# S5 parameters, attention keys, gate rows and S5 copies moved to other places in a hybrid attention and S5 layer

## Chip, cores and metric

The kernel runs on one core of a Trainium2 chip. The metric is the device time of one execution in microseconds (us). The engines are TensorE (PE), VectorE (DVE), ScalarE (ACT), GpSimd (POOL) and SyncE (SP, which issues DMAs). Each works through its own instructions in order and waits on semaphores for the others.

## The reference

One layer of a streaming encoder on 1024 prompt tokens and 64 sample tokens, width 1024, everything in float32. Cut to its steps:

```python
mod = silu(c) @ w_mod + b_mod                      # 1024 x 3072
shift, scale, gate = mod[:, :D], mod[:, D:2*D], mod[:, 2*D:]
h = rms_norm(x, g_norm) * (1 + scale) + shift
z = h @ w_in                                       # 11 column groups
zq, zk, zv, zqi, zki, zwi, zga, zu, zgs, zma, zmb = split_cols(z)
score = sum over heads of wi * relu(qi . ki)       # index scores, rotated qi, ki
keep the top n_sel (256, or 144 for the sample) admissible keys per query
o = softmax(q . k / 8 over the kept keys) @ v      # 8 heads, 2 key heads
branch_a = (o * silu(zga)) @ w_attn_proj
y_ssm, state = s5(zu, lambda, dt, b, c, d_skip)    # complex diagonal scan
g = gelu(y_ssm) @ w_glu                            # 512 -> 1024
branch_b = (g[:, :512] * sigmoid(g[:, 512:]) * silu(zgs)) @ w_ssm_proj
merged = sigmoid(zma) * branch_a + sigmoid(zmb) * branch_b
y = rms_norm(x + gate * (merged @ w_out), g_final)
```

## The kernel before

Every product in float32 is made of three: both operands are split into a rounded high part and the rest (`hhi`, `hlo`, `whi`, `wlo`), and PE adds hi by hi, lo by hi and hi by lo (`mm3_parts`, L197 to L206). A weight split is a DMA into one of two `raw` buffers, a cast on ACT and a subtract on POOL or DVE (`load_split`, L157; `rest_on[0]` says which).

The stages follow each other as PE runs them:

1. **Modulation** (to about 33 us). `w_mod` comes in sixteen slabs. Seven of them are split (`wmh` on ACT, `wml` on DVE), the others are multiplied as they are. The columns of `gate` are left for later.
2. **Turn** (to 107 us). Each of nine token tiles is normed, transposed, scaled (`ht`), split into `hhi` and `hlo` (the subtract of `hlo` on POOL, L557), and projected to index keys (`chunk_a`). `ssm_params`, a generator, works out the S5 parameters in small steps on DVE; before, `next(params, None)` takes one step per tile from tile 2 on.
3. **Index scores and top-k** (to about 277 us on DVE). DVE finds a threshold for each query by counting, makes a mask (`bias`) and flags for blocks that need an exact selection. PE adds up the flags (L948), DVE turns the sum into `arm_i`, and a branch runs `select` for such a block. PE meanwhile runs `kv` and the projection `jobs`: `late` is the queue of these jobs, each of three chunks of 384, 384 and 320 tokens (`products`). Four are queries (`q_d`), four are S5 inputs (`u_d`), then the merge gates (`ma_d`, `mb_d`), and so on. Before, `N_TOPK = 18` steps of `late`, each half a chunk, are run ahead of `topk`, and `beside[0] = gates()` takes one step of the gate product after each chunk: 32 matmuls with the columns of `gate` (L1156).
4. **Attention** (to about 552 us). `build_keys` transposes and splits the keys (`kst`), `att_queries` fetches the first block of queries. Attention is woven with `late`, one step for each of its own (`R_ATT`).
5. **S5** (to about 670 us). `ssm_in` makes the local states `zs`, `ssm_scan` (DVE) runs the scan, `ssm_fix` adds the carries and copies the last states to `fin`, `ssm_out_tables` and `ssm_out` make the outputs. It is woven with `late` at 3.2 steps for each of its own.
6. **Rest of `late`, GLU, branch projections, output.** GLU weights come in pairs by `load_pair`; the result goes to `yhi` and `ylo`. POOL makes `olo` at the start of the GLU (L1516).

The chunks of `late` end in one of two accumulator banks (`acc`, two buffers), which ACT empties (`st`, L609). A scheduler places each engine's instructions, so the order below is its order and not that of the source.

Of the kernel before, what the change touches and what calls it, by code (L numbers as in the profile page):

```python
# [24 lines left out]
F32 = mybir.dt.float32  # L25
# [25 lines left out]
N_TOPK = 18  # L51
# [12 lines left out]
MB = 3  # L64
PAR0 = 2
# [15 lines left out]
def hybrid_step(ctx, tc, ins, outs):  # L81
# [108 lines left out]
    beside = [None]  # L190
# [125 lines left out]
    def ssm_params(sp):  # L316
# [88 lines left out]
        doublings(a8re, a8im, 0)  # L405
        yield
# [262 lines left out]
    ix_ctx = ExitStack()  # L669
# [7 lines left out]
    scores[8] = ixp.tile([P, 576], F32, tag="scs", name="scs", bufs=1)  # L677

    relu_turn = [0]
    sums = ixp.tile([P, 2, 7], F32, name="sums", bufs=1)  # L680
# [85 lines left out]
    def k_of(b):  # L766
        return K_SEL - extra.get(b, 0)
# [80 lines left out]
    tkc = ixp.tile([P, 6, 7], F32, name="tkc", bufs=1)  # L848
    tks = ixp.tile([P, 10, 7], F32, name="tks", bufs=1)
    near_v = ixp.tile([P, 7, NEAR], F32, name="near_v", bufs=1)  # L850
    iota = ixp.tile([P, NEAR], F32, name="iota", bufs=1)
    flags = ixp.tile([P, 14], F32, name="flags", bufs=1)
    fl = ixp.tile([1, 4, 14], F32, name="fl", bufs=1)
    arm_i = ixp.tile([1, 1], I32, name="arm_i", bufs=1)
    ones = ixp.tile([P, 1], F32, name="ones", bufs=1)
    low_f = ixp.tile([P, 1024], BF16, name="low_f", bufs=1)

    def topk_constants():
# [24 lines left out]
        pool.memset(tks[64:P, 9, 6:7], -(bias_w[8] - k_of(8)) * BIG)  # L883
        pool.memset(near_v[64:P, 6], 0.0)

    def topk():
# [14 lines left out]
        for p in range(N_COUNT):  # L901
            now, old = e[p % 2], e[(p + 1) % 2]
            for b in BLOCKS:
                nq, n, i = tok_tile(b)[1], bias_w[b], COL[b]
                c = slice(i, i + 1)
                m = ixp.tile([P, 1024], BF16, tag="gt", name="gt", bufs=2)[:nq, :n]
                dve.tensor_scalar(m, scores[b][:nq], t[:nq, c], -(k_of(b) - (NEAR + 1) / 2), op0=OP.is_ge, op1=OP.add,
                                  accum_out=now[:nq, c])
                if p == N_COUNT - 1:
                    y = ixp.tile([P, 1024], F32, tag="relu", name="below")[:nq, :n]  # L910
# [21 lines left out]
        oh = ixp.tile([P, 7, NEAR], F32, name="oh", bufs=1)  # L932
# [21 lines left out]
        gt = ixp.tile([P, 1024], BF16, tag="gt", name="gts", bufs=2)  # L954
        rk = ixp.tile([P, 1024], F32, tag="relu", name="rank")
# [36 lines left out]
    def att_queries(b):  # L992
        t0, nq = tok_tile(b)

        qt = atp.tile([P, 4, P], F32, tag="qt", name="qt", bufs=1)
        sync.dma_start(qt[:, :, :nq], q_d[:, :, t0:t0 + nq].rearrange("m p t -> p m t"))
        tab = atp.tile([P, 2, P], F32, tag="tab", name="tab", bufs=1)
# [7 lines left out]
        st = atp.tile([P, 4, 2, P], F32R, tag="qs", name="qs")  # L1005
# [133 lines left out]
    run(chunks_b)  # L1139
    inadmissible()  # L1140
    def gates():


        yield
        ps = big()
        for h in range(0, D, 512):
            for k in range(0, KD, 2):
                whi = wpool.tile([P, 2, 512], F32R, tag="whi", name="ghi")
                wlo = wpool.tile([P, 2, 512], F32R, tag="wlo", name="glo")
                v = w_mod[k * P:(k + 2) * P, 2 * D + h:2 * D + h + 512].rearrange("(k p) c -> p k c", p=P)  # L1150
                for i in range(2):
                    load_split(whi[:, i:i + 1], wlo[:, i:i + 1], v[:, i:i + 1])
                yield
                for i in range(2):
                    for j, w in enumerate((whi, wlo)):
                        pe.matmul(ps[0:4, h:h + 512], c4[:, k + i, :], w[:, i], start=(k + i + j == 0),  # L1156
                                  stop=(k + i + j == KD))
                yield
        r = wpool.tile([4, D], F32, tag="whi", name="grow")
        act.copy(r, ps[0:4])  # L1160
        sync.dma_start(grow_d, r)
        for h in range(0, D, 512):
            hs = slice(h, h + 512)
            g = wpool.tile([2, 2, 512], F32, tag="wlo", name="gsum")
            sync.dma_start(g[:, 0:2], grow_d[:, hs].rearrange("(i b) c -> b i c", b=2))
            pool.tensor_tensor(g[:, 0], g[:, 0], g[:, 1], op=OP.add)
            sync.dma_start(g[:, 1], ins["b_mod"][:, 2 * D + h:2 * D + h + 512].to_broadcast([2, 512]))
            pool.tensor_tensor(g[:, 0], g[:, 0], g[:, 1], op=OP.add)
            sync.dma_start(gate_d[:, hs], g[:, 0])
        yield  # L1170
# [9 lines left out]
    beside[0] = gates()  # L1180
# [6 lines left out]
    run(topk())  # L1187
    rest_on[0] = pool
    run(beside[0])
    ix_ctx.close()  # L1190

# [3 lines left out]
    kst = rb.tile([P, 2, 2, 1024], F32R, tag="t2", name="kst")  # L1195

    qw = wpool.tile([P, 4, P], F32, tag="ub", name="qw", bufs=1)
    pool.memset(qw, 0.0)

    def heads():  # L1200
        pt = tokp.tile([P, 2, 2, 4, 2, P], F32R, tag="wtok", name="pt")
        build_keys(kst, None, [(ktok[:, t], P) for t in range(8)])
        keys, vals = kst, [vst]
        with tc.issue_after(q_stored.ins):
            ready = att_queries(BO[0])
        other = None
        for i, b in enumerate(BO):
            if b == 8:
                ck = atp.tile([P, 4, P], F32, tag="qt", name="ck", bufs=1)
# [4 lines left out]
            for h in range(8):  # L1214
# [4 lines left out]
                if h == VH and b == 8:  # L1219
                    cv = atp.tile([P, 4, 2, 64], F32, tag="qt", name="cv", bufs=1)  # L1220
# [58 lines left out]
    act.mul(arf[:, 1, 16:32], a8im, -1.0)  # L1279
    ca_t, tq_t = {}, {}  # L1280

    def ssm_out_tables(q):
# [101 lines left out]
    def ssm_fix(q):  # L1384
# [98 lines left out]
    rest_on[0] = dve  # L1483
    nxt = load_pair(*pairs[0])
# [184 lines left out]
```

## Time and profile before

| | us |
|---|---|
| median of 3 runs (1076.43 to 1077.16) | 1077.0 |
| profiled execution | 1080.46 |
| its span (first to last instruction) | 1077.8 |
| PE busy | 989.8 |
| DVE busy | 660.6 |
| ACT busy | 497.5 |
| POOL busy | 314.6 |

The times of all rows come from the one profiled execution and count from its span's start. A row of a timeline gives the start, the duration, the engine, the line, the operation, output and inputs, the shape, and in brackets how long the engine was idle before it and what ended that. Instructions of one engine overlap a little, so that the step from one start to the next says what one costs in a row of equal ones. Lines are those of the kernel before.

### The profile page before, as it was taken

The numbers are of one execution on the slowest core, as the hardware profiler recorded it, in microseconds if no ns is written. First come the engines' busy times: TensorE is split into PE (matmuls) and PEld (weight loads), VectorE is DVE, ScalarE is ACT, GpSimd is POOL, SyncE is SP. The second block draws the span as 40 slices with busy tenths as digits, with TensorE's granted clock in tenths as the row PEclk, the third lists the DMA queues.
The fourth block names the chain that finished last, engine by engine and source line by source line (L and its number), as shares of the span: only waits on it lengthen the run. The fifth ranks groups of instructions, "written<-read, shape, count | busy, mean of one in ns | idle before, by whom it ended". The sixth has DMA issues, their size and how long they took to land. (4 is left out here: it accounts for less than half of the span.)

```text
span 1077.8 us, 16668 instructions
## 1 busy us (share of the span) xinstructions
PE 989.8 (92%) x5910; PEld 893.7 (83%) x5910; DVE 660.6 (61%) x1478; ACT 497.5 (46%) x1034; POOL 314.6 (29%) x456
## 2 busy tenths in 40 slices
PE   7766999999979999999989948999899999999997
PEld 1565777998868899998878947999899999998786
DVE  3596888899278788876556996110323566564243
ACT  3654577322269778887614102223431344442122
POOL 2565102444454312211142715533123000001200
PEclk9887999999999899999999987999999999999999
DMA  8711301134533212113293304465432345444133
GB/s 307 213 51 55 89 1 47 40 92 130 124 80 78 69 33 58 48 54 87 42 154 82 98 11 121 121 143 115 158 107 93 89 153 164 145 121 156 52 129 113
DMA packets 142009, 108.43 MB, mean 101 GB/s; under 512 B 33126, under 2 KB 128912, under 8 KB 141924
## 3 DMA queue, kind: packets, MB, share of 16 engines
q1 hardware_dynamic: 140404, 105.08, 35.1%
q10 hardware_dynamic: 1232, 2.23, 0.6%
q8 instruction: 46, 0.75, 0.3%
q14 instruction: 39, 0.32, 0.1%
q0 software_dynamic: 288, 0.05, 0.0%
HBM read 77.81 MB, written 25.19 MB: 96 GB/s over the span
## 5 line engine op out<-in xcount | busy, mean ns | idle before, releaser
L200 PE MATMUL acc<-hhi,whi 128*128 128x384 f32 (+1 forms) x768 | 259.3, 342 | 10.0 <-ACT whi L154 4.0
L201 PE MATMUL acc<-hlo,whi 128*128 128x384 f32 (+1 forms) x768 | 255.8, 337 | 0.0
L205 PE MATMUL acc<-hhi,wlo 128*128 128x384 f32 (+1 forms) x768 | 150.4, 335 | 14.8 <-POOL wlo L155 14.8
L200 PEld LDWEIGHTS acc<-hhi,whi 128*128 128x128 f32 x768 | 148.6, 193 | 13.5 <-ACT whi L154 4.6
L201 PEld LDWEIGHTS acc<-hlo,whi 128*128 128x128 f32 x768 | 148.7, 194 | 1.3 <-issue 0.4
L205 PEld LDWEIGHTS acc<-hhi,wlo 128*128 128x128 f32 x768 | 131.0, 191 | 16.7 <-POOL wlo L155 15.7
L155 POOL TENSOR_TENSOR wlo<-raw,whi 128x512 fp32r<-128x512 f32 x64 | 91.3, 1441 | 179.8 <-ACT whi L154 143.8
L609 ACT COPY st<-acc 128x384 f32<-128x384 f32 (+1 forms) x60 | 27.5, 459 | 93.2 <-PE acc L205 76.5
L154 ACT CAST whi<-raw 128x512 fp32r<-128x512 f32 x64 | 38.4, 620 | 56.7 <-PE acc L205 23.9
L1069 DVE TENSOR_TENSOR pt<-tp,pt 128x512 fp32r<-128x512 f32 (+3 forms) x112 | 56.6, 520 | 12.3 <-ACT pt L1068 10.8
L1604 POOL TENSOR_TENSOR yh<-yh,gfin 128x512 f32<-128x512 f32 (+1 forms) x9 | 11.6, 1287 | 174.5 <-ACT xr L1600 174.5
L1040 ACT ACTIVATE pm<-pm,mx 128x1024 f32<-128x1024 f32 (+8 forms) x72 | 56.0, 779 | 12.5 <-DVE mx L1033 12.3
L1030 PE MATMUL sc<-kst,qs 128*128 128x512 f32 (+3 forms) x192 | 54.8, 364 | 4.8 <-issue 4.4
L200 PE MATMUL acc<-wohi,mhi 128*128 128x512 f32 (+2 forms) x152 | 57.8, 384 | 0.0
L201 PE MATMUL acc<-wolo,mhi 128*128 128x512 f32 (+2 forms) x152 | 57.5, 383 | 0.0
L1064 PE MATMUL tp<-ident,pm 128*128 128x128 f32 (+2 forms) x328 | 53.4, 272 | 2.6 <-DVE pm L1048 1.5
L1033 DVE CUSTOM_DVE_ANT_0 pm<-sc,bias 128x512 f32<-128x512 f32 (+4 forms) x72 | 43.1, 598 | 18.5 <-PE sc L1030 15.1
L1068 ACT CAST pt<-tp 128x512 fp32r<-128x512 f32 (+3 forms) x112 | 48.8, 450 | 12.2 <-PE tp L1064 10.8
L1081 PE MATMUL o<-pt,vst 128*128 128x256 f32 x288 | 49.0, 296 | 2.4 <-ACT pt L1068 1.6
L1064 PEld LDWEIGHTS tp<-ident,pm 128*128 128x128 f32 (+2 forms) x328 | 38.6, 140 | 12.1 <-issue 5.2
L705 DVE SCALAR_TENSOR_TENSOR sc<-relu,wi,sc 128x512 f32<-128x512 f32 (+5 forms) x42 | 43.2, 1031 | 4.1 <-ACT relu L703 1.3
L1081 PEld LDWEIGHTS o<-pt,vst 128*128 128x128 f32 x288 | 40.3, 192 | 6.5 <-DVE pt L1069 2.7
(476 smaller groups left out, 2271.6 us busy)
## 6 DMA issues: line engine op xcount, KB each, us to landing
raw<-in_w_in SPq DMA_DIRECT2D x68, 256.0 KB
wm<-in_w_mod SPq DMA_DIRECT2D x16, 512.0 KB
xt<-in_x_prompt SPq DMA_DIRECT2D x8, 512.0 KB
raw<-in_w_mod SPq DMA_DIRECT2D x16, 256.0 KB
raw<-in_w_out SPq DMA_DIRECT2D x16, 256.0 KB
xr<-in_x_prompt SPq DMA_DIRECT2D x16, 256.0 KB
ma_d<-st SPq DMA_DIRECT2D x16, 192.0 KB
mb_d<-st SPq DMA_DIRECT2D x16, 192.0 KB
```

Of the source, the lines that this page charges most:

```text
L155: rest_on[0].tensor_tensor(lo, raw, hi.bitcast(F32), op=OP.subtract)
L200: pe.matmul(ps, lhi(k), rhi(k), start=(k == 0), stop=False)
L201: pe.matmul(ps, lhi(k), rlo(k), start=False, stop=False)
L205: last_mm[0] = pe.matmul(ps, llo(k), rhi(k), start=False, stop=(k == nk - 1))
L705: dve.scalar_tensor_tensor(scores[b][:nq], r[:nq, :n], w, scores[b][:nq], op0=OP.mult, op1=OP.add, accum_out=sums[:nq, 0, col] if h == 4 e ...
L1030: pe.matmul(ps, self.st[:, self.h // 2, self.h % 2, :nq], self.keys[:, self.h // 4, j, c:c + m], start=(j == 0), stop=(j == 1))
L1033: dve.tensor_tensor_reduce(out=self.pm[:, c:c + m], in0=ps, in1=bias[self.b][:nq, c:c + m], op0=OP.add, op1=OP.min, scale=-0.125, scalar=t ...
L1040: act.activation(self.pm, self.pm, AF.Exp, bias=self.ng, scale=-1.0, accum_out=self.sm)
L1064: pe.transpose(tp[:rows, i, :nq], self.pm[:, c0:c0 + rows], ident[:nq, :nq])
L1068: act.copy(d0, tp[:rows, i0:i1, :nq])
L1069: dve.tensor_tensor(d1, tp[:rows, i0:i1, :nq], d0.bitcast(F32), op=OP.subtract)
L1081: last_mm[0] = pe.matmul(o, v[:rows, kt, pr // 2].rearrange("p a d -> p (a d)"), pk[:rows, j, i, :, :nq], start=(kt == 0 and j == 0), stop ...
```

## The change

Four parts. The parameters' first three steps run within the modulation loop (`PARK`), and the DMA of the S5 matrices becomes a step of its own. `N_TOPK` is 0, and the keys and first queries are made ahead of the branch, in pools of their own. The gate product leaves the chunks and runs in the GLU loop, two steps for each chunk, one 128 x 512 slab per step. In the S5 stage the copies to `fin` go from POOL to ACT, a memset from POOL to DVE, and the second half of `ca` from DVE to POOL.

```diff
-N_TOPK = 18
+N_TOPK = 0
+PARK = (1, 2, 3)
...
                 evac(c, t0, n, ps)
-                if beside[0]:
-                    next(beside[0], None)
...
             if 2 * k + 1 - j == X0:
                 load_x(0)
+        if k in PARK:
+            next(params)
...
+    def gates(gp):
+        ps = [bank1()[0:4], bank1()[0:4]]
+        parts = [(h, k) for h in range(2) for k in range(KD)]
+        def load(h, k):
+            w = [gp.tile([P, 1, 512], F32R, tag=f"gw{i}", name=f"gw{i}") for i in range(2)]
+            load_split(w[0], w[1], w_mod[k * P:(k + 1) * P, None, 2 * D + h * 512:2 * D + h * 512 + 512])
+            return w
+        nxt = load(*parts[0])
+        yield
+        for i, (h, k) in enumerate(parts):
+            w, nxt = nxt, load(*parts[i + 1]) if i + 1 < len(parts) else None
+            for j in range(2):
+                pe.matmul(ps[h], c4[:, k, :], w[j][:, 0], start=(k + j == 0), stop=(k + j == KD))
+            yield
...
-    run(topk())
+    tk = topk(ixp)
+    for _ in range(N_COUNT - 1 + len(BLOCKS) + 1):
+        next(tk)
+    qw = wpool.tile([P, 4, P], F32, tag="ub", name="qw", bufs=1)
+    pool.memset(qw, 0.0)
+    kst = rb.tile([P, 2, 2, 1024], F32R, tag="t2", name="kst")
+    build_keys(kst, None, [(ktok[:, t], P) for t in range(8)])
+    with tc.issue_after(q_stored.ins):
+        ready = att_queries(BO[0])
+    run(tk)
     rest_on[0] = pool
-    run(beside[0])
...
-        dve.scalar_tensor_tensor(ca[:, :, 1], u1, -1.0, u2, op0=OP.mult, op1=OP.subtract)
+        pool.tensor_tensor(ca[:, :, 1], u1, u2, op=OP.subtract)
...
-        pool.tensor_copy(fin[:, 1, :, rs], z4[:, :, rs, 8])
-        pool.tensor_copy(fin[:, 0, :, rs], z4[:, :, rs, NCH])
-        pool.memset(z4[:, :, rs, 8], 0.0)
+        act.copy(fin[:, 1, :, rs], z4[:, :, rs, 8])
+        act.copy(fin[:, 0, :, rs], z4[:, :, rs, NCH])
+        dve.memset(z4[:, :, rs, 8], 0.0)
...
     rest_on[0] = dve
+    gate_gen = gates(ga_ctx.enter_context(tc.tile_pool(name="gap", bufs=2, side="right")))
     nxt = load_pair(*pairs[0])
...
             dve.tensor_tensor(ylo[:, m, t0:t0 + n], s[:, :n], yhi[:, m, t0:t0 + n].bitcast(F32), op=OP.subtract)
+            for _ in range(2):
+                next(gate_gen, None)
...
+    run(gate_gen)
```

PE's order at the flags matmul, before; the last of sixteen chunks since `kv` stands ahead of it, the gate matmuls (L1156) around it, and the transposes of the keys behind it:

```order
L205 MATMUL acc<-hhi,wlo 128x320 x8
L948 MATMUL acc<-flags,ones 1x14
L200 MATMUL acc<-hhi,whi 128x384
L201 MATMUL acc<-hlo,whi 128x384
L1156 MATMUL big<-ghi,c_128 4x512
L961 UNCONDITIONAL_BRANCH
```

The same place in the change, where it is the tenth chunk that stands ahead:

```order
L205 MATMUL acc<-hhi,wlo 128x320 x8
L989 MATMUL tp<-ident,ktok 128x128 x8
L950 MATMUL acc<-flags,ones 1x14
L200 MATMUL acc<-hhi,whi 128x384
L201 MATMUL acc<-hlo,whi 128x384
```

The key transposes have come ahead of the flags, and six chunks and all gate matmuls have gone behind them or further.

POOL's order in the S5 stage, before, from the table's last products to the second copies to `fin` (each pair of `wlo` is one job's weights):

```order
L155 TENSOR_TENSOR wlo<-raw,whi 128x512 x2
L1293 TENSOR_TENSOR u_8400<-par 128x576
L1400 COPY fin<-zs 128x2x4
L1401 COPY fin<-zs 128x2x4
L1402 MEMSET zs 128x2x4
L155 TENSOR_TENSOR wlo<-raw,whi 128x512 x2
L1400 COPY fin<-zs 128x2x4
```

ACT's order in the change, from the seventh evacuation of a chunk after the last local state to the tenth:

```order
L610 COPY st<-acc 128x384 x2
L610 COPY st<-acc 128x320
L1411 COPY fin<-zs 128x2x4
L1412 COPY fin<-zs 128x2x4
L155 CAST whi<-raw 128x512 x2
L610 COPY st<-acc 128x384
L1411 COPY fin<-zs 128x2x4
```

The copies have left POOL's row of `wlo` and stand in ACT's row of evacuations and casts; POOL's row of `wlo` has none between.

SP's loads in the first half of the GLU, before:

```order
L161 DMA raw<-in_w_glu 128x4x128 x2
L1505 DMA gs<-gs_d 128x384 x2
L161 DMA raw<-in_w_glu 128x4x128 x2
L1505 DMA gssg<-gs_d 128x320
L1505 DMA gs<-gs_d 128x384 x2
```

And in the change:

```order
L162 DMA raw<-in_w_mod 128x512 x2
L1518 DMA gs<-gs_d 128x384
L162 DMA raw<-in_w_mod 128x512 x2
L1518 DMA gs<-gs_d 128x384
L162 DMA raw<-in_w_mod 128x512 x2
L162 DMA raw<-in_w_glu 128x4x128 x2
```

Six loads of gate weights stand ahead of the GLU's next pair, and all of them use the two `raw` buffers.

## Rows read from the trace of the kernel before

**Rows 1.** The page's first part: busy us, share of the span, instructions.

```profile
PE 989.8 (92%) x5910; PEld 893.7 (83%) x5910; DVE 660.6 (61%) x1478; ACT 497.5 (46%) x1034; POOL 314.6 (29%) x456
```

**Rows 2.** Table of stretches: length, busy us of each engine, granted PE clock, DMA.

```profile
core 0: us, PE busy (x) PEld busy (x) DVE busy (x) ACT busy (x) POOL busy (x), PEclk, DMA share, GB/s
6.00:31.00 25.00, 24.49 (x61) 3.53 (x62) 8.58 (x7) 7.57 (x9) 2.66 (x7) 1.00 0.95 342
52.00:100.00 48.00, 35.48 (x241) 32.78 (x241) 41.23 (x150) 27.24 (x63) 31.12 (x91) 0.86 0.19 54
640.00:680.00 40.00, 29.32 (x164) 27.40 (x165) 24.34 (x31) 7.01 (x14) 23.16 (x37) 0.75 0.44 111
```

**Rows 3.** Timeline of DVE, modulation and turn stage.

```profile
25.20 1.23 DVE L483 TENSOR_TENSOR wml<-wm,wmh 128x1024 fp32r<-128x1024 f32 x1 [1.81 <-ACT wmh L482]
...
53.22 0.17 DVE L283 TENSOR_SCALAR sv<-sv 128x16 f32<-128x16 f32 x1
53.42 2.39 DVE L284 TENSOR_SCALAR sv<-sv 128x16 f32<-128x16 f32 x1
```

**Rows 4.** Timeline of POOL, turn stage.

```profile
53.40 2.39 POOL L557 TENSOR_TENSOR hlo<-ht,hhi 128x1024 fp32r<-128x1024 f32 x1 [1.83 <-ACT hhi L556]
```

**Rows 5.** Timeline of PE, the end of the turn stage, the flags, the first score.

```profile
103.22 0.37 PE L587 MATMUL tp<-ident,zA 64*128 64x64 f32 x1 [5.35 <-POOL zA L243]
...
295.14 0.20 PE L948 MATMUL acc<-flags,ones 128*1 128x14 f32 x2
...
311.53 3.65 PE L1030 MATMUL sc<-kst,qs 128*128 128x512 f32 x8 [4.42 <-issue]
```

**Rows 6.** Timeline of DVE, the end of the top-k.

```profile
270.73 1.01 DVE L942 SCALAR_TENSOR_TENSOR bias<-sc,tks,nbig 128x768 bf16<-128x768 f32 x1
...
271.67 2.17 DVE L942 SCALAR_TENSOR_TENSOR bias<-sc,tks,nbig 128x896 bf16<-128x896 f32 x1
...
276.85 0.17 DVE L944 TENSOR_TENSOR flags<-tks,tkc 128x7 f32<-128x7 f32 x1
295.38 0.16 DVE L950 SCALAR_TENSOR_TENSOR fl<-acc,fl 1x14 f32<-1x14 f32 x1 [18.36 <-PE acc L948]
```

**Rows 7.** Timeline of ACT, evacuations of projection chunks while PE never waits.

```profile
806.74 0.48 ACT L609 COPY st<-acc 128x384 f32<-128x384 f32 x1 [3.79 <-PE acc L205]
810.96 0.48 ACT L609 COPY st<-acc 128x384 f32<-128x384 f32 x1 [3.75 <-PE acc L205]
...
814.48 0.43 ACT L609 COPY st<-acc 128x320 f32<-128x320 f32 x1
```

**Rows 8.** Timeline of PE, gate matmuls.

```profile
290.82 0.40 PE L1156 MATMUL big<-glo,c 128*4 128x512 f32 x1
291.06 0.40 PE L1156 MATMUL big<-ghi,c 128*4 128x512 f32 x1
```

**Rows 9.** Timeline of DVE, the start of the S5 stage.

```profile
554.94 0.83 DVE L1297 SCALAR_TENSOR_TENSOR ca<-u,u 128x576 f32<-128x576 f32 x1 [4.15 <-POOL u L1296]
```

**Rows 10.** Timeline of PE, its waits in the S5 stage.

```profile
556.42 0.88 PE L1342 MATMUL tp<-ident,eb 128*128 128x128 f32 x6 [4.21 <-DVE eb L278]
...
646.86 3.36 PE L205 MATMUL acc<-hhi,wlo 128*128 128x384 f32 x8 [14.77 <-POOL wlo L155]
653.97 0.69 PE L200 MATMUL acc<-hhi,whi 128*128 128x384 f32 x1 [3.75 <-ACT st L609]
```

**Rows 11.** Timeline of POOL, the first copy to fin.

```profile
643.84 0.62 POOL L1400 COPY fin<-zs 128x8 f32<-128x8 f32 x1 [14.65 <-DVE zs L1399]
```

**Rows 12.** Timeline of ACT in the S5 stage, the ninth evacuation.

```profile
617.39 0.43 ACT L609 COPY st<-acc 128x320 f32<-128x320 f32 x1 [3.03 <-PE acc L205]
```

**Rows 13.** SP's queue, a load through a raw buffer.

```profile
899.49 0.33 SPq L161 DMA_DIRECT2D raw<-in_w_out  x1
```

**Rows 14.** Timeline of DVE: the subtracts at the GLU's start, and that of the load above.

```profile
826.51 6.02 DVE L155 TENSOR_TENSOR wlop<-raw,whip 128x512 fp32r<-128x512 f32 x2 [10.68 <-ACT whip L154]
...
903.17 0.69 DVE L155 TENSOR_TENSOR wolo<-raw,wohi 128x512 fp32r<-128x512 f32 x1 [0.62 <-ACT wohi L154]
```

**Rows 15.** Timeline of POOL, the GLU's start.

```profile
826.50 11.24 POOL L1516 TENSOR_TENSOR olo<-oT,ohi 128x1088 fp32r<-128x1088 f32 x4 [21.32 <-PE acc L205]
```

More of the change, by code (lines that the diff above doesn't have):

```diff
@@ L405, in ssm_params @@
         doublings(a8re, a8im, 0)
+        yield
+        braw = scr[:, 0:1].rearrange("p o (j r c) -> p (o j) r c", j=2, r=16)
+        craw = scr[:, 1:2].rearrange("p o (j a c) -> p (o j) a c", j=2, a=4)
+        with tc.issue_after(last_w.ins):
+            for j, nm in enumerate(("ssm_b_re", "ssm_b_im")):
+                sync.dma_start(braw[:, j], ins[nm][0].rearrange("(r g) p c -> (g p) r c", g=2))
+            for j, nm in enumerate(("ssm_c_re", "ssm_c_im")):
+                sync.dma_start(craw[:, j], ins[nm][0].rearrange("(a g) c p -> (g c) a p", g=8))
         yield
@@ L676, in hybrid_step @@
         off += bias_w[b]
-    scores[8] = ixp.tile([P, 576], F32, tag="scs", name="scs", bufs=1)
+    scores[8] = tkp.tile([P, 576], F32, name="scs")
     relu_turn = [0]
-    sums = ixp.tile([P, 2, 7], F32, name="sums", bufs=1)
+    sums = tkp.tile([P, 2, 7], F32, name="sums")
     COL = {2: 0, 3: 1, 4: 2, 5: 3, 6: 4, 7: 5, 8: 6}
@@ L846, in gauss @@
         return z, math.exp(-z * z / 2) / math.sqrt(2 * math.pi)
[L848 to L856, printed above, removed]
+    tkc = tkp.tile([P, 6, 7], F32, name="tkc")
+    tks = tkp.tile([P, 10, 7], F32, name="tks")
+    iota = tkp.tile([P, NEAR], F32, name="iota")
+    flags = tkp.tile([P, 14], F32, name="flags")
+    fl = tkp.tile([1, 4, 14], F32, name="fl")
+    arm_i = tkp.tile([1, 1], I32, name="arm_i")
+    ones = tkp.tile([P, 1], F32, name="ones")
     def topk_constants():
@@ L883, in topk_constants, with topk @@
         pool.memset(tks[64:P, 9, 6:7], -(bias_w[8] - k_of(8)) * BIG)
+    def topk(tky):
+        near_v = tky.tile([P, 7, NEAR], F32, name="near_v", bufs=1)
         pool.memset(near_v[64:P, 6], 0.0)
-    def topk():
         t, s, g, e0, e1, u, w, j, v, acc_m = (tks[:, i] for i in range(10))
@@ L909, in topk @@
                 if p == N_COUNT - 1:
-                    y = ixp.tile([P, 1024], F32, tag="relu", name="below")[:nq, :n]
+                    y = tky.tile([P, 1024], F32, tag="y", name="below")[:nq, :n]
                     dve.scalar_tensor_tensor(y, m, LOW, scores[b][:nq], op0=OP.mult, op1=OP.add)
@@ L931, in topk @@
         dve.tensor_scalar(j, now, -1.0, (NEAR + 1) / 2, op0=OP.mult, op1=OP.add)
-        oh = ixp.tile([P, 7, NEAR], F32, name="oh", bufs=1)
+        oh = tky.tile([P, 7, NEAR], F32, name="oh", bufs=1)
         sh = [P, 7, NEAR]
@@ L953, in topk @@
         dve.scalar_tensor_tensor(arm_i, sm[:, 1:2], 8.0, sm[:, 2:3], op0=OP.min, op1=OP.add)
-        gt = ixp.tile([P, 1024], BF16, tag="gt", name="gts", bufs=2)
-        rk = ixp.tile([P, 1024], F32, tag="relu", name="rank")
+        gt = tky.tile([P, 1024], BF16, tag="gt", name="gts")
+        low_f = tky.tile([P, 1024], BF16, tag="gt", name="low_f")
+        rk = tky.tile([P, 1024], F32, tag="y", name="rank")
+        for z in (gt, low_f, rk):
+            pool.memset(z[0:1, 0:1], 0.0)
         arm = nc.vector.value_load(arm_i[0:1, 0:1], min_val=0, max_val=9)
@@ L1004, in att_queries @@
         pool.tensor_tensor(qt[:, :, :nq], qt[:, :, :nq], qw[:, :, :nq], op=OP.add)
-        st = atp.tile([P, 4, 2, P], F32R, tag="qs", name="qs")
+        st = atq.tile([P, 4, 2, P], F32R, tag="qs", name="qs")
         stack_queries(st, qt, 4, 4, nq)
@@ L1132, in hybrid_step @@
             next(chunks_b)
+    run(chunks_b)
+    ix_ctx.close()
+    ixp = ix_ctx.enter_context(tc.tile_pool(name="tky", bufs=2, side="right"))
     bias_all = kv1.tile([P, sum(bias_w)], BF16, tag="bz", name="bias")
@@ L1138, in hybrid_step @@
     topk_constants()
-    run(chunks_b)
     inadmissible()
-    def gates():
-        yield
[L1145 to L1164, printed above, removed]
+    def gates(gp):
[6 more added lines that the diff above has]
+        nxt = load(*parts[0])
+        yield
+        for i, (h, k) in enumerate(parts):
[3 more added lines that the diff above has]
+            yield
+        for h in range(2):
+            hs = slice(h * 512, h * 512 + 512)
+            r = gp.tile([4, 512], F32, tag="gw0", name="grow")
+            act.copy(r, ps[h])
+            sync.dma_start(grow_d[:, hs], r)
+            g = gp.tile([2, 2, 512], F32, tag="gsum", name="gsum", bufs=1)
@@ L1179, in hybrid_step @@
     kvs = kv()
-    beside[0] = gates()
     run(kvs)
@@ L1194, in hybrid_step @@
     oT = rb.tile([P, 4, TOK], F32, tag="t1", name="oT")
-    kst = rb.tile([P, 2, 2, 1024], F32R, tag="t2", name="kst")
-    qw = wpool.tile([P, 4, P], F32, tag="ub", name="qw", bufs=1)
-    pool.memset(qw, 0.0)
     def heads():
+        nonlocal ready
         pt = tokp.tile([P, 2, 2, 4, 2, P], F32R, tag="wtok", name="pt")
-        build_keys(kst, None, [(ktok[:, t], P) for t in range(8)])
         keys, vals = kst, [vst]
-        with tc.issue_after(q_stored.ins):
-            ready = att_queries(BO[0])
         other = None
@@ L1208, in heads @@
             if b == 8:
-                ck = atp.tile([P, 4, P], F32, tag="qt", name="ck", bufs=1)
+                ck = atq.tile([P, 4, P], F32, tag="qt", name="ck", bufs=1)
                 sync.dma_start(ck, ins["cache_k"][0, 0].rearrange("(a p) g d -> p a (g d)", p=P))
@@ L1279, in hybrid_step @@
     act.mul(arf[:, 1, 16:32], a8im, -1.0)
+    ncr = ssp.tile([P, 16, 16], F32, name="ncr")
+    act.mul(ncr, cc[:, 0], -1.0)
     ca_t, tq_t = {}, {}
```

30 lines of the change are left out of this document (14 added, 16 removed).

## The prediction

> **What bounds the kernel now.** I read the page's busy times first. TensorE (PE) is busy for 92% of the span [rows 1], so a change gains only where it removes idle PE time or time at the lower clock, and it loses wherever it adds either. PE work that is only moved costs its full price again at its new place if PE is busy there. So I went through the table of stretches [rows 2], and then through the timelines for what ends each wait, at the four places that the diff touches.
>
> The turn stage (52 to 100 us) has PE busy for 35.5 of 48 us at a granted clock of 0.86, with DVE the fullest engine there (41.2 us) [rows 2]. At the top-k, DVE has its last flag at 277.0, but PE comes to the flags matmul only at 295.14, so DVE waits 18.36 us [rows 5, 6]. In the SSM stage PE waits 14.77 us for wlo [rows 10]. At the GLU PE has no wait.
>
> **The profiled execution and the median.** The profiled execution took 1080.5 us (1077.8 of span and 2.7 around it), 3.5 above the median of 1077.0. My terms are differences within its trace. I add them to the median, since 0.3% of a few us is nothing.
>
> **S5 parameters beside the modulation.** About 100 small DVE instructions leave the turn stage. One of them alone takes 0.17 us, but 2.39 us where POOL's subtract of hlo runs [rows 3, 4]; five such meetings, each 2.2 us too long, are 11 us, and 100 at 0.1 to 0.2 us from start to start are 10 to 20. So some 27 of DVE's 41.2 us go. POOL, with 31.1 us, is then the fullest, so the stretch of 48 us can lose at most 17. Not all of it goes, because ACT, POOL and PE hand a tile on in turn; I take 10 (4 to 17). The wait of 5.35 us at 103.22 stays: POOL's constants for the top-k stand after the last hlo in both orders [rows 5].
>
> The same instructions now stand between DVE's seven splits of the modulation weights, where DVE is busy for 8.6 of 25 us [rows 2]. Ahead of each split DVE idles about 1.8 us [rows 3]. The order puts 9, 17, 22 and 25 of them between the later splits, 2 to 5 us each time, so the last splits come 1 to 6 us late. PE needs the last one only near its end; I take 3.4 us (0 to 7). Together this part gives **-6.6** (-15 to +3).
>
> **Keys and queries ahead of the branch, and N_TOPK = 0.** In the order of before, sixteen projection chunks and most gate matmuls stand ahead of the flags matmul; in the order of the change ten chunks, the key transposes, and nothing else. A chunk of 384 columns costs 4.22 us of PE, one of 320 3.52 [rows 7], so PE is done some 24 us of chunks, 7 us of gates and 4 us of waits for gate weights sooner, near 260. DVE isn't, so PE now waits for DVE. DVE's end moves from 277.0 to about 273, since the gates' POOL splits no longer stretch its two-input instructions (one of 896 columns took 2.17 us where 768 took about 1.0; there are five or six such) [rows 6]. From flags to the first attention score it is 16.4 us now [rows 5]; the branch stays, and only one of eight key pieces moves ahead of it, so 15.7. The scores start at 289 instead of 311.5, 22.8 us sooner. But PE has then done 5.2 chunks (20.6 us) and all gate matmuls (32 of 0.235 us from start to start, 7.5 us [rows 8]) less, and nothing shows idle PE later that would take them: the weaves of attention and SSM draw as many chunks as before, and the rest runs at a PE that is never idle. Add 1.2 us, since the 10.9 us of chunks behind the flags start at the lower clock after a wait of 13 us. The part costs 28.1 - 22.8 + 1.2 = **+6.5**. If DVE is not relieved at all it is 10.5; if the branch costs 4 us less with the keys ready, 2.5.
>
> **S5 copies off POOL.** Two things. First, the VectorE instruction that waited 4.15 us for POOL [rows 9] is gone, and with it PE's wait of 4.21 us for eb [rows 10]: -4.2. Second, POOL no longer holds wlo behind the copies to fin, which wait for DVE until 643.84 [rows 11]. But ACT holds them now, in order. Ahead of the first copy it has nine evacuations, as the one at 617.39 is the ninth [rows 12]; behind it stand the cast of whi and the tenth evacuation. There are two accumulator banks, so PE can do chunks 10 and 11, until about 626, and then waits until ACT has copied fin (643.8), cast whi (1.2) and evacuated (0.5): a wait of 20 us in the place of 14.77 and 3.75. Chunks 12 to 14 are still to do then, where before it was one and a third. The lower clock after the wait (0.75 over 640 to 680 [rows 2]; eight matmuls took 3.36 us at 646.86 [rows 10]) falls on these. I get the first ssm_out some 3 us later against the scan than before. DVE's scan sets both, so the sum is **-1** (-12 if nothing waits behind the copies, +5 if the clock stays low longer).
>
> **Gate rows beside the GLU.** The matmuls are counted above. New is that 16 loads of 256 KB go through the two raw buffers in which the GLU's own weights arrive, while PE meets the gate matmuls in its order from the second chunk to the ninth. A raw buffer turns round in 4.4 us: issue at 899.49, subtract done at 903.86 [rows 13, 14]. Up to the ninth chunk 22 loads are due, eleven turns or 48 us, against some 43 us of PE work. Worse, POOL's four subtracts for olo run over the first 11.2 us of the stage, and two DVE subtracts there took 6.0 us instead of 1.4 [rows 14, 15], so the first gate pair is ready about 9.7 us into the stage, where PE asks for it at 4.6 and 5.2. Following both buffers from turn to turn, I get PE waits of 2.2 and 2.3 us at the first pair, 1.2 at the third, and 1.3 twice behind the GLU's own pairs, with small ones between: **+9** (4 to 14). Only a page gives another price for the load: the Trainium skill (SBUF — State Buffer, The DMA setup-cost knee) fits 2 us and the bytes at 436 GB/s, an estimate of 2.6 us where the row here has about 3.0 with its issue. By it a turn would be 4.0 us and this term about 5.
>
> The sum is -6.6 + 6.5 - 1 + 9 = +7.9, so **1085 us**.
>
> **Rivals.**
> - *The waits don't form, and it is faster.* ACT's copies or the raw buffers don't hold PE as I draw it: DVE's scan ends sooner with POOL's copies gone, or the loads run ahead during the last projection. For it: POOL's wlo is what PE waits for now [rows 10, 11], and POOL no longer waits. Against it: the copies wait for the same DVE instruction wherever they stand. It decides if the wait at 646.86 falls below 8 us. Then S5 copies give -10 instead of -1, and with the GLU at 4 the sum is -6: 1071 (1064 to 1075).
> - *The terms cancel.* The turn stage gives the whole 17 us, which needs DVE's contention to have been the only brake there; the sum is +1: 1078.
> - *A deeper loss.* The modulation is 7 us late and DVE not relieved at the top-k: +15, 1092. The Trainium skill (SBUF — State Buffer, Who interferes with whom) has the pair of ports that DVE and GpSimd share held by whoever issues first, with the other blocked for the whole instruction. By that rule the gate splits on DVE, which meet olo, could also come first and make olo wait instead. This trace agrees with the blocking (2.39 us on both engines, [rows 3, 4]), and in the modulation POOL is busy for only 2.7 of 25 us [rows 2], which speaks against this rival's first half.
>
> **How the numbers follow.** My forecast has 0.53, the faster rival 0.27, cancelling 0.12, the deeper loss 0.08. The likeliest is 1085 on its own range of 1080 to 1090. For 8 in 10 the range reaches from 1068 (part of the faster rival, which has the nearest bounds) to 1093. A measurement here tells about 0.2% (2 us) from no change. Faster is 0.28, the same 0.13, slower 0.59.
>
> **What the profile after would show.** PE in 52 to 100 busy for over 42 us; the last modulation split near 29. One PE wait of 11 to 16 us ahead of the flags matmul, and first scores some 20 us sooner. No PE wait for eb; a PE wait of about 20 us released by ACT st in the SSM stage, none by POOL wlo. In the GLU, PE waits released by gw0 and gw1. I am wrong if the SSM wait is gone, or if the GLU has less than 4 us of waits.

## The result

The changed kernel takes 1089.66 us (median of 4 runs, 1088.23 to 1090.05) where the kernel before takes 1076.83 (median of 4, 1076.43 to 1077.16): ratio 1.0119 with the interval [1.0092, 1.0146], 12.8 us slower. The forecast was 1085, slower, with a range of 1068 to 1093.

### The profile after

The page's first part, as [rows 1]:

```profile
PE 989.2 (91%) x5910; PEld 891.7 (82%) x5910; DVE 664.0 (61%) x1494; ACT 498.4 (46%) x1044; POOL 293.9 (27%) x435
```

PE does the same work in the same time, 989.2 us against 989.8, in a span of 1088.2 us instead of 1077.8. What was lost is idle PE time. Table of stretches after, as [rows 2], with the S5 scan and the GLU added:

```profile
core 0: us, PE busy (x) PEld busy (x) DVE busy (x) ACT busy (x) POOL busy (x), PEclk, DMA share, GB/s
6.00:31.00 25.00, 24.59 (x63) 3.81 (x64) 18.09 (x84) 6.85 (x9) 3.67 (x11) 1.00 0.89 315
52.00:100.00 48.00, 36.76 (x267) 33.58 (x266) 26.54 (x58) 30.88 (x70) 35.35 (x140) 0.93 0.19 54
580.00:640.00 60.00, 37.39 (x214) 35.79 (x213) 48.75 (x121) 8.56 (x24) 18.48 (x18) 0.80 0.23 62
820.00:885.00 65.00, 59.91 (x337) 53.65 (x336) 41.72 (x58) 27.18 (x53) 13.84 (x6) 0.97 0.46 143
```

In the turn stage DVE falls from 41.2 to 26.5 us as drawn, but PE goes only from 35.5 to 36.8: POOL, now busy for 35.4 of 48 us, is the fullest beside PE. Timeline of PE after, the longer waits, as [rows 5, 10]:

```profile
97.64 0.43 PE L588 MATMUL tp<-ident,zA 128*128 128x128 f32 x1 [3.80 <-POOL zA L241]
271.20 0.21 PE L950 MATMUL acc<-flags,ones 128*1 128x14 f32 x2 [16.09 <-DVE flags L946]
284.68 1.56 PE L1035 MATMUL sc<-kst,qs 128*128 128x512 f32 x6
516.25 0.87 PE L1353 MATMUL tp<-ident,eb 128*128 128x128 f32 x6 [1.01 <-DVE eb L276]
520.20 0.41 PE L1353 MATMUL tp<-ident,eb 128*128 128x128 f32 x2 [1.84 <-DVE eb L273]
524.49 1.54 PE L1353 MATMUL tp<-ident,eb 128*128 128x128 f32 x6 [1.10 <-DVE eb L276]
540.52 3.04 PE L1360 MATMUL big<-uall,eq 128*64 128x136 f32 x32 [2.33 <-ACT eq L1354]
611.72 0.64 PE L200 MATMUL acc<-hhi,whi 128*128 128x320 f32 x1 [19.33 <-ACT st L610]
625.45 0.44 PE L200 MATMUL acc<-hhi,whi 128*128 128x384 f32 x1 [2.88 <-ACT st L610]
828.33 0.40 PE L1162 MATMUL tp<-gw,c 128*4 128x512 f32 x1 [2.04 <-ACT gw L155]
830.81 0.39 PE L1162 MATMUL tp<-gw,c 128*4 128x512 f32 x1 [1.74 <-DVE gw L156]
```

PE now waits 16 us for DVE's flags where DVE waited 18 us for PE. The first score comes 26.9 us sooner (284.68 against 311.53). In the S5 stage 14.77 and 3.75 us of waits have become 19.33 and 2.88, and in the GLU there are waits for the gate weights.

The best single view of all this is PE's idle time by stage, the sum of the brackets of its timeline. The stages end with the first index score, the first attention score, the first transpose of `eb`, the first S5 output product and the first GLU product; the last column runs to the end of the kernel. A wait that ends with such a mark is counted in the stage that the mark begins, as the 4.42 us ahead of the first score before [rows 5]. The experiments' rows are explained below.

| kernel | head | top-k | attention | S5 | outputs, late | GLU | all | ratio to before |
|---|---|---|---|---|---|---|---|---|
| before | 28.8 | 9.9 | 9.6 | 25.2 | 5.5 | 0 | 79.0 | 1 |
| changed | 25.6 | 20.4 | 3.0 | 29.3 | 7.2 | 5.1 | 90.5 | 1.0119 |
| p1_params | 25.7 | 9.6 | 9.7 | 24.6 | 4.8 | 0 | 74.4 | 0.9942 |
| p2_keys | 29.8 | 25.2 | 5.8 | 25.8 | 8.8 | 0 | 95.4 | 1.0179 |
| p3_gates | 26.4 | 4.1 | 10.5 | 24.4 | 5.5 | 5.3 | 76.3 | 0.9994 |
| p4_s5 | 29.1 | 8.8 | 8.5 | 31.5 | 6.5 | 0 | 84.5 | 1.0041 |
| a_topk12 | 25.8 | 8.0 | 12.7 | 28.3 | 11.1 | 5.9 | 91.8 | 1.0123 |
| a_topk18 | 25.5 | 11.3 | 6.9 | 31.1 | 5.2 | 5.2 | 85.1 | 1.0071 |
| a_findve | 25.3 | 20.0 | 3.6 | 29.6 | 8.0 | 5.2 | 91.7 | 1.0095 |
| a_ownraw | 25.5 | 20.5 | 2.4 | 30.2 | 7.4 | 5.0 | 90.9 | 1.0093 |
| b_extra | 27.9 | 8.7 | 10.0 | 25.4 | 6.6 | 0 | 78.5 | 1.0010 |
| a_extra | 24.7 | 21.6 | 3.5 | 30.5 | 5.8 | 6.6 | 92.7 | 1.0102 |
| p1_extra | 25.5 | 9.0 | 9.7 | 25.2 | 6.5 | 0 | 75.9 | 0.9969 |
| p1_zq3 | 24.0 | 8.2 | 8.7 | 10.4 | 7.7 | 0 | 59.0 | 0.9854 |

The change adds 11.5 us of idle time, and the span grew by 10.4. Of one and the same code, the head differs by up to 2.7 us from profile to profile (26.4 in `p3_gates`, 29.1 in `p4_s5`), so differences under 3 us in one place of this table mean nothing by themselves. Nor is idle time all of it: for the same 5910 matmuls PE is busy for 981.7 us in `p1_params` and 995.1 in `p2_keys`, at a mean granted clock of 0.971 and 0.953.

### The profile page after: what moved, and what is told of

The parts are those of the page before. It is cut to its first block, busy times and chain, and to the rows that moved or that the text cites. A ratio compares the mean times of both kernels' runs of the same rounds, so it can differ in the third digit from the quotient of the medians.

```text
span 1088.2 us, 16695 instructions
## 1 busy us (share of the span) xinstructions
PE 989.2 (91%) x5910; PEld 891.7 (82%) x5910; DVE 664.0 (61%) x1494; ACT 498.4 (46%) x1044; POOL 293.9 (27%) x435
## 4 chain that ended last, share of the span: by engine, by line
PE 56%; DVE 22%; ACT 8%; issue 5%; DMA 4%; POOL 3%; SPq 1%; POOLq 0%; ACTq 0%; DVEq 0%
PE acc L200 11%; PE acc L201 11%; PE acc L205 11%; PE big L205 3%; PE sc L1035 3%; PE big L201 3%; PE big L200 3%; PE o L1086 2%; PE tp L1069 2%; DMA raw<-in_w_in 2%; DVE gt L909 2%; DVE near_v L916 2%; DVE sc L708 1%; DVE t L1368 1%; PE big L695 1%
## 5 line engine op out<-in xcount | busy, mean ns | idle before, releaser
L156 POOL TENSOR_TENSOR wlo<-raw,whi 128x512 fp32r<-128x512 f32 x64 | 86.8, 1374 | 226.9 <-ACT whi L155 184.1
L619 DVE TENSOR_TENSOR sg<-acc,sg 128x384 f32<-128x384 f32 (+1 forms) x12 | 6.3, 534 | 103.9 <-ACT sg L618 96.0
L1035 PE MATMUL sc<-kst,qs 128*128 128x512 f32 (+3 forms) x192 | 52.1, 351 | 0.0
L1038 DVE CUSTOM_DVE_ANT_0 pm<-sc,bias 128x512 f32<-128x512 f32 (+4 forms) x72 | 42.9, 596 | 14.8 <-PE sc L1035 12.9
```

Of the source, the lines that this page charges most:

```text
L156: rest_on[0].tensor_tensor(lo, raw, hi.bitcast(F32), op=OP.subtract)
L1035: pe.matmul(ps, self.st[:, self.h // 2, self.h % 2, :nq], self.keys[:, self.h // 4, j, c:c + m], start=(j == 0), stop=(j == 1))
L1038: dve.tensor_tensor_reduce(out=self.pm[:, c:c + m], in0=ps, in1=bias[self.b][:nq, c:c + m], op0=OP.add, op1=OP.min, scale=-0.125, scalar=t ...
```

## The experiments

### The four parts alone

Each is the kernel before with one part of the change. `p1_params` has the `PARK` steps and the moved DMA; `p2_keys` has `N_TOPK = 0` and the keys and queries ahead of the branch, with the gate product still beside the chunks; `p3_gates` has the gate product in the GLU; `p4_s5` has the copies to `fin` on ACT, the memset on DVE and `ca` on POOL.

> The kernel before with the S5 parameters beside the modulation alone. If the four parts add up stage by stage, the first index score comes 4 us sooner as in the changed kernel and nothing later gives that back: ratio near 0.996. Rival: the head's gain is taken back later, where PE waits for DVE anyway (the flags): ratio 1.000.

> The kernel before with the keys and first queries ahead of the branch and N_TOPK = 0 alone; the gate matmuls stay beside the chunks. If PE work is only put off, the first score comes 17 to 20 us sooner, the rest of the projections takes about 20 us more and the ratio is 1.000 (0.997 to 1.005). Rival: the earlier start of the attention is worth its time: ratio 0.985.

> The kernel before with the gate rows in the GLU alone. If the two raw buffers hold up PE, the GLU takes 15 us more (7.5 of matmuls, 8 of waits and lower clock), the stage from 240 to 300 us 12 less (7.5 and 5 of waits): ratio 1.003 (1.000 to 1.006). Rival: the loads are hidden in the GLU, and the 5 us of waits in the projection stage are gone: ratio 0.995.

> The kernel before with the S5 part alone (copies to fin on ACT, memset on DVE, the second half of ca on POOL). If ACT only takes over POOL's wait, PE waits about 19 us for ACT's st in place of 15 for POOL's wlo, and the ratio is 1.005 (1.002 to 1.008). Rival: the loss in this stage of the changed kernel comes from the parts ahead of it, and this part alone gains the 4 us of the wait for eb: ratio 0.996.

Measured: `p1_params` 0.9942 [0.9920, 0.9964], `p2_keys` 1.0179 [1.0140, 1.0219], `p3_gates` 0.9994 [0.9977, 1.0011], `p4_s5` 1.0041 [1.0018, 1.0063]. Part 1 gains, as the theory has it, and keeps it to the end. Part 4 loses by itself, as its theory has it. Part 3 costs nothing alone, between its two expectations: the GLU grows by 16.4 us, but the top-k stage shrinks by 12.9, of which 7.5 are the gate matmuls that left it, and the attention by 5.8, for which no run shows the cause. Part 2 alone fell outside both expectations. Its timelines of POOL and PE in the top-k:

```profile
251.45 0.09 POOL L959 MEMSET gts<- 1x1 bf16 x1 [3.87 <-DVE below L912]
262.32 0.09 POOL L959 MEMSET rank<- 1x1 f32 x1 [10.78 <-DVE near_v L915]
263.82 0.09 POOL L959 MEMSET low_f<- 1x1 bf16 x1 [1.42 <-DVE below L912]
263.94 2.73 POOL L155 TENSOR_TENSOR glo<-raw,ghi 128x512 fp32r<-128x512 f32 x2
...
265.41 0.59 PE L1162 MATMUL big<-glo,c 128*4 128x512 f32 x1 [13.94 <-POOL glo L155]
```

Three memsets of one element each, which the new pools need, wait for buffers that DVE's top-k still reads. Behind them in POOL's queue stands the split of the gate weights, and PE waits 13.94 us for that. The first score comes at 312.42, no sooner than before. So keys ahead pays nothing as long as weights are split on POOL behind those memsets, and part 3 takes these splits away; the pair of parts 2 and 3 was not run by itself. The four alone add up to -6.2, +19.3, -0.6 and +4.4 us, 16.9, against 12.8 together.

### How much chunk work belongs ahead of the flags

```diff
-N_TOPK = 0
+N_TOPK = 12
```

and `N_TOPK = 18` in a second kernel, in the changed kernel.

> The changed kernel with N_TOPK = 12: four chunks stand ahead of the flags matmul that fill PE's wait of 16 us there. If that wait is paid in full, it falls below 2 us with the first score at the same time; but the order leaves only two us of chunks between flags and first score, so a wait of some 11 us comes there instead: 5 to 8 us faster than the changed kernel, ratio to before 1.006. Rival: PE is late at the flags again and the first score moves back by as much as the chunks cost: ratio 1.012, as the changed kernel.

> The changed kernel with N_TOPK = 18 again, so that only the place of the keys and queries is left of this part. PE comes to the flags some 8 us after DVE has its last flag, first score near 293, about five chunks more done by then than in the changed kernel: 8 to 10 us faster than it, ratio 1.003. Rival: an early start of the attention is what counts: 8 us slower than the changed kernel, ratio 1.019.

Measured: 1.0123 [1.0080, 1.0167] and 1.0071 [1.0051, 1.0091]. With 12 the wait of 16 us at the flags is gone, and nothing is won: the time is the rival's, but not for its reason, since the first score doesn't move back. PE and DVE in that kernel:

```profile
288.06 1.22 PE L1035 MATMUL sc<-kst,qs 128*128 128x512 f32 x2 [9.56 <-DVE kst L268]
...
286.74 1.26 DVE L268 CAST kst<-kst 64x512 fp32r<-64x512 f32 x1 [2.58 <-issue]
```

The first score comes at 276.6, but PE then stands for a key piece that DVE can only split behind the branch; the scheduler left seven of DVE's eight instructions for the keys there. That wait, 9.56 us, is the one of some 11 us that the theory named. A further 5.65 us of waiting appear at the first S5 outputs, and all idle time is 91.8 us against 90.5. With 18 it is 85.1, and the time follows (-5 us), between the two expectations and nearer to the theory, which had 8 to 10: the top-k stage idles for 9.1 us less and the attention for 3.9 more, of which PE waits 4.52 for a key piece from DVE. So filling the wait at the flags was worth some 5 us at most and not 16, because DVE, through the keys, is what is late next. Why 18 steps gain and 12 don't isn't settled.

### Who makes the last copies of the S5 states

```diff
-        act.copy(fin[:, 1, :, rs], z4[:, :, rs, 8])
-        act.copy(fin[:, 0, :, rs], z4[:, :, rs, NCH])
+        dve.tensor_copy(fin[:, 1, :, rs], z4[:, :, rs, 8])
+        dve.tensor_copy(fin[:, 0, :, rs], z4[:, :, rs, NCH])
```

> The changed kernel with the copies to fin on DVE, behind the additions that they wait for. If PE's wait of 19.3 us comes from ACT's row alone, it goes, PE does its fourteen chunks during the scan and the first ssm_out moves from 85 to about 70 us behind the start of the scan: 12 to 16 us faster than the changed kernel, ratio near 1.000. Rival: the outputs wait for DVE's scan or for POOL's tables in any case, and PE waits there instead: no more than 5 us faster, ratio 1.008.

Measured: 1.0095 [1.0065, 1.0125], nearer to the rival. The copies now stand on the engine that makes the states, where no split and no evacuation waits behind them, and PE's wait is as long as ever. Timelines of PE, ACT and SP in this kernel:

```profile
621.40 0.69 PE L200 MATMUL acc<-hhi,whi 128*128 128x384 f32 x1 [21.49 <-ACT st L610]
...
618.06 0.62 ACT L155 CAST whi<-raw 128x512 fp32r<-128x512 f32 x1 [25.33 <-DMA raw<-in_w_in]
...
586.95 0.38 SPq L162 DMA_DIRECT2D raw<-in_w_in  x1
613.21 1.26 SPq L1421 DMA_DIRECT2D zq<-zs  x2
614.58 0.55 SPq L162 DMA_DIRECT2D raw<-in_w_in  x1
```

And the longest of SP's waits from 585 to 632 us (engine, line, what it waited for: us in total, times, longest):

```profile
SPq L1421 <- DVE zs L1413: 25.8, 1, 25.8
```

SP issues nothing for 26 us, because at the head of its queue stands the load of `zq`, which waits for the first corrected states. Behind it stand the raw loads and stores of the projection chunks, which need nothing of the scan. ACT's cast waits 25.33 us for one of these loads, and the evacuation that PE waits for stands behind the cast. SP's waits had it all along, from 560 to 670 us in the kernel before:

```profile
SPq L1410 <- DVE zs L1399: 22.0, 1, 22.0
```

and from 530 to 640 us in the changed one:

```profile
SPq L1421 <- DVE zs L1413: 23.0, 1, 23.0
```

POOL before and ACT in the change did hold PE as the prediction drew it, in their own queues:

```profile
645.10 3.42 POOL L155 TENSOR_TENSOR wlo<-raw,whi 128x512 fp32r<-128x512 f32 x2
...
609.94 0.20 ACT L1411 COPY fin<-zs 128x8 f32<-128x8 f32 x1 [25.69 <-DVE zs L1410]
```

The first line is from the kernel before, behind the copies that began at 643.84 [rows 11]; its inputs had been cast by 622.2. The second is from the changed one. But each was only one of two holders that let go at about the same time, since the copies and the `zq` load wait for the same states. As long as SP holds the loads, moving the copies from one engine to another gains nothing, and this run shows it.

### Raw buffers of its own for the gate product

```diff
-            load_split(w[0], w[1], w_mod[k * P:(k + 1) * P, None, 2 * D + h * 512:2 * D + h * 512 + 512])
+            raw = gp.tile([P, 1, 512], F32, tag="graw", name="graw")
+            sync.dma_start(raw, w_mod[k * P:(k + 1) * P, None, 2 * D + h * 512:2 * D + h * 512 + 512])
+            split(w[0], w[1], raw)
```

> The changed kernel with two raw buffers of their own for the gate loads. If the shared buffers hold up the gate pairs, PE's waits in the GLU fall from 5 us to 2 (what is left is DVE's splits beside POOL's olo): 3 to 6 us faster than the changed kernel, ratio 1.008. Rival: olo's hold on DVE makes all of the wait: no change, ratio 1.012.

Measured: 1.0093 [1.0059, 1.0128], between the two, and its interval overlaps that of the change. The GLU itself is no shorter (62.6 us against 62.8) and its waits are 5.0 us against 5.1. Timelines of ACT, DVE and PE at the GLU's start:

```profile
822.56 0.62 ACT L155 CAST gw<-graw 128x512 fp32r<-128x512 f32 x1 [2.53 <-DMA graw<-in_w_mod]
...
819.61 6.00 DVE L156 TENSOR_TENSOR wlop<-raw,whip 128x512 fp32r<-128x512 f32 x2 [10.67 <-ACT whip L155]
825.53 2.96 DVE L156 TENSOR_TENSOR gw<-graw,gw 128x512 fp32r<-128x512 f32 x1
...
828.55 0.59 PE L1164 MATMUL tp<-gw,c 128*4 128x512 f32 x1 [4.63 <-DVE gw L156]
```

The weights now arrive in time (cast at 822.56), but DVE's subtract can't start before 825.53: two GLU subtracts stand in front of it, and they take 6.0 us beside POOL's `olo`. In the changed kernel the first load did come late, in ACT's timeline:

```profile
827.66 0.62 ACT L155 CAST gw<-raw 128x512 fp32r<-128x512 f32 x1 [5.38 <-DMA raw<-in_w_mod]
```

So the raw buffers were a brake of the GLU, but taking it off gains nothing that can be told from noise, because DVE is as late: PE's one wait of 4.63 us stands in the place of 2.04 and 1.74.

### Taking the chunks out from behind the zq load

First, in both kernels and with part 1 alone, five empty steps of the weave after the scan, so that more chunks are emitted ahead of the first correction:

```diff
+        for _ in range(5):
+            yield
         for q in range(4):
             ssm_fix(q)
             yield
```

> The kernel before with five empty steps of the weave between the end of the scan and the first correction of the S5 states, so that some 16 more steps of late chunk work (3.2 to a step) stand ahead of the first zq load in every queue; nothing else is changed. Theory: the 18.5 us in which TensorE waits there come from SyncE's queue, where the first zq load waits 22.0 us for the corrected states and the raw loads and stores of the chunks stand behind it; with more chunks ahead of that load TensorE works through the scan, the wait all but goes, and as the number of chunks is fixed the late stage is shorter by as much: ratio about 0.984 (0.980 to 0.990). Rival, the reading of the prediction: the wait is that of the engine that makes the copies of the corrected states (GpSimd before, ScalarE after), so that chunk work put ahead only moves it: ratio 1.000 (0.997 to 1.003).

> The changed kernel with the same five empty steps ahead of the first correction. Theory: the 19.33 us wait goes by some 16 to 18 us, and ratio to the kernel before falls from 1.012 to about 0.996 (0.992 to 1.000). Rival: the copies on ScalarE hold it, 1.012 (1.009 to 1.015).

> The kernel before with the S5 parameters beside the modulation (part 1 of the change alone) and the five empty steps. Theory: the two gains add, 0.994 with 0.984, about 0.978 (0.973 to 0.984). Rival: the steps bring nothing, 0.994 (0.991 to 0.997).

Measured: 1.0010 [0.9983, 1.0037], 1.0102 [1.0069, 1.0136] and 0.9969 [0.9951, 0.9988]. All three went to the rival. PE and SP in `b_extra`:

```profile
642.08 3.36 PE L205 MATMUL acc<-hhi,wlo 128*128 128x384 f32 x8 [14.65 <-POOL wlo L155]
...
613.60 0.79 SPq L161 DMA_DIRECT2D raw<-in_w_in  x1
640.37 1.26 SPq L1410 DMA_DIRECT2D zq<-zs  x2
642.05 0.39 SPq L161 DMA_DIRECT2D raw<-in_w_in  x1
```

But the edit didn't do what it was for. PE did do more chunks in the S5 stage (21.5 instead of 16.2), but only behind the wait. The scheduler had put the first `zq` load behind the same raw load as before, whatever the source emits ahead of it, and SP waited 21.9 us there. POOL's copies to `fin`, too, stood ahead of the same `wlo` as before. So the expectation failed because of the order, and the mechanism was still open. The last kernel forces the order. It is part 1 with three empty steps, the copies to `fin` and the memset on DVE, and

```diff
-        for j in range(2):
-            for g2 in range(2):
-                sync.dma_start(zq[64 * j:64 * j + 64, :, g2, :], ...)
+        with tc.issue_after(stored[0].ins):
+            for j in range(2):
+                for g2 in range(2):
+                    sync.dma_start(zq[64 * j:64 * j + 64, :, g2, :], ...)
```

where `stored[0]` is the last store of a chunk so far.

> Part 1 alone, with three empty steps between the scan and the first correction, the copies of the corrected states on VectorE, and each zq load queued on SyncE behind the last chunk store that the program has emitted by then (in the kernels before, the scheduler put the first zq load ahead of stores and raw loads that the program emits before it, and the empty steps alone left it there). Theory, with both parts of the blocked queue undone: SyncE no longer holds the chunks' raw loads for the scan, the 14.7 us and 3.4 us waits of part 1 alone go to under 3 us together, and what is done there is missing from the late stage: ratio about 0.980 (0.975 to 0.986), against 0.994 for part 1 alone. Rival: VectorE, not the queue, is what the stage lacks, the waits form again at another place (the first S5 output products, or the chunks' evacuation): 0.994 (0.990 to 0.998).

Measured: 0.9854 [0.9815, 0.9894], 1059.18 us. It is faster than both kernels. The theory's direction and place hold; the size is a little short of the expected 0.980, but within its range of 0.975 to 0.986. PE's longest wait of the scan, in its timeline:

```profile
629.57 0.69 PE L201 MATMUL acc<-hhi,whi 128*128 128x384 f32 x1 [3.37 <-ACT st L613]
```

and SP's first `zq` loads, and its longest waits from 560 to 670 us:

```profile
649.60 2.60 SPq L1415 DMA_DIRECT2D zq<-zs  x4
...
SPq L614 <- ACT st L613: 33.9, 12, 5.7
SPq L162 <- POOL wlo L156: 25.7, 12, 11.7
```

The wait of 22 us for `zs` is off SP's list: fourteen more loads and stores of chunks stand ahead of `zq`. PE's wait of 14.74 us in `p1_params` is gone, and the S5 stage has 10.4 us of idle PE time instead of 24.6. PE does 3.3 more chunks than there in a stage that is 3.1 us shorter, and the late stage is 8.0 us shorter. Not all of the idle time comes back as time: all of it is 15.4 us less than in `p1_params`, but PE is busy for 989.7 us instead of 981.7. The `zq` order was not run without the copies on DVE, nor the copies without the order on this base. `b_extra` (the kernel before) and `a_findve` (the changed one) show that neither the steps nor the copies alone move the wait; whether the order alone does is open.

## Why the prediction was right, and where not

The sign, the four places and the range were right. That the sum of +8 came as near to 12.8 as it did is in part luck: two terms were off by 6 and 8 us in opposite directions. Stage lengths are from one mark to the next in the two profiles; by them the four parts make +10.7, and the spans of the two profiled executions differ by 10.4. The medians differ by more, since the profiled execution before took 3.5 us more than its median, and the one after 0.4.

**S5 parameters: -6.6 predicted, -4.4 at the first index score in the changed kernel, -6.3 in `p1_params`.** The modulation's last split ends 3.0 us later (29.4), close to the 3.4 taken. The turn stage gives 7.4 and not 10, and PE in 52 to 100 us is busy for 36.8 us and not over 42, the one sign of this part that did not come. DVE's relief was as drawn, and POOL was next: from 30 us to the first index score PE waits 9.1 us for `zA` where it waited 7.7, the longest 3.80, and 1.4 for `hlo` where it had no such wait.

**Keys and queries: +6.5 predicted, +0.4 measured.** The scores are sooner by 22.5 us after the 4.4 of part 1 (22.8 predicted), and here two errors cancel: DVE was relieved by 1.6 us and not 4 (its flags are done at 271.05, the 4.4 of part 1 included), but from the flags to the first score it is 13.5 us where I had 15.7. The outputs and the late stage are longer by 25.0 us, with 6.0 more chunks (of 24 matmuls), and the gate matmuls are 7.5. What the step "nothing shows idle PE later that would take them" missed is the attention stage, 9.6 us shorter: 0.8 chunks less there are some 3.3 us, idle time inside the stage is 2.3 less, and the other 4 go with the clock (granted 1.00 over the stage, where it was 0.98). So -22.5 - 9.6 + 25.0 + 7.5 = +0.4. The bound of 2.5 that I had given for a branch that costs 4 us less came nearer, but it had nothing of the attention in it.

**S5 copies: -1 predicted, +6.8 measured** (from the first `eb` transpose to the first output product, 120.2 us against 113.4). With the same 16.2 chunks, 4.1 of it are idle time and 2.6 go with the lower clock (0.86 over the stage, where it was 0.88). The size is not sharp: with the same S5 code the stage takes 118.2 us in `a_ownraw`, and in `p4_s5` it is 3.4 longer than before. The wait of 20 us released by ACT's `st` came as drawn (19.33), but ACT's later copies made another of 2.88 behind it that the sum didn't have. The step that failed is the gain of 4.2 at `eb`. The DVE instruction that waited for POOL is gone, but POOL now makes both halves of `ca`, and its products for them run beside DVE's products for `eb`, where DVE had stood idle before. Timelines of DVE and POOL after:

```profile
518.59 1.46 DVE L273 TENSOR_TENSOR eb<-v,v 128x512 f32<-128x512 f32 x1
520.09 2.05 DVE L274 TENSOR_TENSOR v<-par 128x512 f32<-128x512 f32 x1
522.06 1.65 DVE L275 TENSOR_TENSOR v<-par 128x512 f32<-128x512 f32 x1
523.74 0.69 DVE L276 TENSOR_TENSOR eb<-v,v 128x512 f32<-128x512 f32 x1
...
519.47 0.73 POOL L1322 TENSOR_TENSOR dd<-par 32x64 f32<-32x64 f32 x1
520.17 1.42 POOL L1308 TENSOR_TENSOR ca<-u,u 128x576 f32<-128x576 f32 x1
521.66 1.50 POOL L1304 TENSOR_TENSOR u<-par 128x576 f32<-128x576 f32 x1
```

A product takes 0.69 us alone and 1.5 to 2.1 beside POOL, until POOL is done at 523.2. PE waits 1.01, 1.84 and 1.10 us for `eb` and 2.33 for `eq`, and all its waits up to the start of the scan come to 6.6 us, where they were 6.7. `p4_s5` has the same, with waits of 1.00, 0.92 and 2.96 us for `eb`. That POOL is the cause is read from the rows; the move of `ca` was not run by itself. The Trainium skill (SBUF — State Buffer, Who interferes with whom) has a DVE instruction with two SBUF inputs contend with a GpSimd instruction that reads SBUF, over a shared pair of ports that is an exclusive lock. These rows agree with it. The prediction reckoned with this contention in the modulation and the GLU and forgot it here.

**Gate rows: +9 predicted, +7.9 measured** (the GLU 15.4 us longer, less the 7.5 of matmuls): 5.1 of waits, of which 2.04, 1.74 and 1.09 are the longest, and a rest of 2.8 that goes with the lower clock behind them (granted 0.97 over the stretch). The size was right, and both of its reasons are there, but one is enough: the first pair's load comes late through the raw buffers, and without their turns (`a_ownraw`) DVE behind `olo` is as late, and the waits are still 5.0 us.

Of the rivals, "the waits don't form" is out: the waits ahead of the flags, in the scan and in the GLU formed at the sizes named. Its condition, POOL no longer holding `wlo`, was met without any gain, because ACT's copies held the evacuations, and without these (`a_findve`) SP held the loads. The prediction had ACT's queue and not SP's.

## What to carry to other kernels

Where an engine waits long for another engine's evacuation, look at what the DMA queue was doing in that time: here one load that waited for late data held the independent loads and stores behind it, and moving work between engines then only renamed the wait. When an edit is to change an order that a scheduler makes, read the new order before the time. Work that is moved ahead of a bottleneck comes back in the stage that it left or later, so idle time of the bound engine, stage by stage, is the sum to forecast, together with its clock.

## What was not expected of the hardware

In `p2_keys` a memset of one element (0.09 us) held GpSimd's queue for 10.78 us, the largest part of TensorE's wait of 13.94, through the reuse of a buffer alone. One DMA issue held SyncE for 22.0 us (before), 23.0 (changed) and 25.8 (`a_findve`), while TensorE's longest wait there was shown as one for GpSimd (14.77) or ScalarE (19.33 and 21.49).
